# Fewer convolution taps behind each attention head group of block two's first layer, the rest behind the linear attention

## The chip, the cores and the metric

The kernel runs on one core of one Trainium2 chip. The metric is the device time of one execution in microseconds (us), as the median of several. The engines named below are TensorE (PE, its weight loads PEld), VectorE (DVE), ScalarE (ACT), GpSimd (POOL), and SyncE (SP), whose queue issues the loads.

## What is computed

Two blocks of two layers each work on a sequence of 256 tokens of width 1024; block two carries a second sequence of 256 context tokens along. The change touches layer 0 of block two. There, three branches read the same normalised input: a convolution of 31 taps over time with 512 channels, a gated linear attention (GLA, in chunks of 64), and a grouped attention of 8 heads. Three sigmoid gates merge them:

```python
def conv_module(val, glu, gate, dw_w, dw_b, ln_g, ln_b, w_o):
    u = val * jax.nn.sigmoid(glu)
    u = lax.conv_general_dilated(u, dw_w[:, None, :], ..., feature_group_count=D_CONV) + dw_b
    u = jax.nn.silu(layer_norm_2(u, ln_g, ln_b)) * jax.nn.silu(gate)
    return u @ w_o
...
    def merge(p, ya, yb, yc):
        return (jax.nn.sigmoid(p[13]) * ya + jax.nn.sigmoid(p[14]) * yb
                + jax.nn.sigmoid(p[15]) * yc) @ w_out
```

## The kernel before

Every product of two matrices is made of three matmuls (lines 163 to 165): weights and activations are split into a high and a low half, and high by high, high by low and low by high are added up in PSUM. A weight unit of 512 KB is loaded by SP into a raw tile (wr), ACT makes its high half (wh, line 133) and DVE its low half (wl, line 134). Units are loaded and split a few ahead of their use.

Layer 0 of block two runs over both sequences at once, 512 tokens. Its program order is: keys, queries and values of the attention; the convolution's inputs (up, four tiles of 128 channels); the attention, in eight groups (four blocks of 128 tokens, named at00 to at03, by two key heads), with the matmuls of GLA's keys, queries and values (f0GK, f0GQ, t0GV) and of the attention's output gate (f0ag) as filler; then the gate ag and the branch m3 with the attention's output weights oa; GLA in two passes (gl00 for the context, gl01 for the sequence); the gate gg and the branch m2 with GLA's output weights og; the end of the convolution (transposes cvt of ucv on, line 1316); the gate cg and the branch m1 with oc.

A branch works through four pairs of gates: two matmul groups f0m, then two output groups (yoa, yog, yoc), each added into acc by DVE. A gate such as gg has four parts; each ends in a product with the branch (qgg, line 1256), split into ygg0 (high, ACT) and ygg1 (low, DVE, line 199), which the matmuls of yog read.

The convolution is 124 DVE instructions in one chain: four tiles ucv of 31 taps, each tap reading and writing the same ucv (lines 989 and 991). They come from a generator, `taps`, and are given out in portions. A portion is only tied to stand behind its anchor, an instruction on the same engine:

```python
    def some_taps(n, anchor):
        for _ in range(n):
            t = next(taps, None)
            if t is not None:
                g.after(t, anchor)
```

The anchors are: for each attention group, the product that puts its row maxima in place (line 1033), with `TAPS[l]` taps; for each part of the gate ag and each merge of m3, `TAPG[l][0]` and `TAPG[l][1]`; for each part of the gate gg and each merge of m2, `TAPG[l][2]` and `TAPG[l][3]`. What is left is given out at the start of `conv_finish`. With 20 behind each group, six groups and a part of the seventh use up all 124, and the other portions of layer 0 find none. A scheduler in the framework fixes each engine's order when the program is built, from priorities that follow the program's order and from its own estimates; on the chip each engine works through its own list in that order.

Of the kernel before, what the change touches and what calls it, by code (L numbers as in the profile page):

```python
# [733 lines left out]

TAPS = (20, 19)
TAPG = ((0, 15, 5, 4), (3, 3, 14, 10))


def mod_stream(g, l, W):
# [74 lines left out]
def block2(g, l, hT, res_of, W, out=None, then=lambda x: None):  # L816
# [177 lines left out]
# [7 lines that stand above are left out]
    def scores(tb, kv):  # L1001
# [18 lines left out]
        for h in range(0, 4, n):  # L1020
# [5 lines left out]
            if h + n < 4:  # L1026
# [5 lines left out]
        nc.tensor.transpose(pm, ms.bitcast(F32).rearrange("p a h -> p (a h)"), idf)  # L1032
        some_taps(TAPS[l], nc.vector.tensor_mul(q2[64:72], pm[:, None, :].to_broadcast([8, 4, 128]),
                                                g.hm[0:8, :, None].to_broadcast([8, 4, 128])))
# [212 lines left out]
    def gate(n, f, q):  # L1247

        ps = fm(f'{n}{f}')
        tg = tgt(f'gt{n}{f}')  # L1250
        nc.scalar.activation(tg, ps, AF.Tanh, scale=0.5, bias=hb[:, blk(n, f)])
        nc.scalar.activation(q[:, f, :], ps, AF.Identity, bias=b_all[:, blk(n, f)])
        nc.vector.scalar_tensor_tensor(q[:, f, :], tg, 1.0, q[:, f, :], op0=OP.add, op1=OP.mult)

    def gated(f, q, src, y, scale, ntaps):
        nc.vector.tensor_mul(q[:, f, :], q[:, f, :], src)
        some_taps(ntaps, split_out(g, y[0][:, f, :], y[1][:, f, :], q[:, f, :], scale))
# [39 lines left out]
    def branch(bi, n, o, y, ntaps):  # L1297
        for i in range(4):
            merge(bi, o, i, [merge_gate(n, 2 * i + mb) for mb in range(2)], y, ntaps)

    def merge_gates(n):
        sg = k8('sg' + n, [128, 8, NT])
        return [merge_gate(n, f, sg[:, f, :]) for f in range(8)]

    def merges(bi, o, sg, y, ntaps):
        for i in range(4):
            merge(bi, o, i, sg[2 * i:2 * i + 2], y, ntaps)

    def conv_finish():
        for _ in taps:  # L1310
            pass
        ns = []
        for tb in range(NT // 128):
            pt = pp.tile([128, 4, 128], F32, name=f'cvt{l}{tb}', tag='at', bufs=g.AT)
            for f in range(4):
                nc.tensor.transpose(pt[:, f, :], ucv[f][:, 128 * tb:128 * tb + 128], idf)
            st = sp.tile([128, 6], F32, name=f'cvs{l}{tb}', tag='cvs', bufs=4)
            nc.vector.bn_stats(st, pt.rearrange("p f t -> p (f t)"))
            mv = sp.tile([128, 2], F32, name=f'cvm{l}{tb}', tag='cvm', bufs=4)
            nc.vector.bn_aggr(mv, st)  # L1320
            y = rsqrt(g, mv[:, 1:2], 1, 1.0, 1e-6, f'cv{l}{tb}')
            n = t2(f'cvn{tb}')
            nc.vector.tensor_scalar(n, pt.rearrange("p f t -> p (f t)"), mv[:, 0:1], y, op0=OP.subtract, op1=OP.mult)
            ns.append(n)
        for f in range(4):
            pt = pp.tile([128, NT], F32, name=f'cvb{l}{f}', tag='at', bufs=g.AT)
            for tb in range(NT // 128):
                nc.tensor.transpose(pt[:, 128 * tb:128 * tb + 128], ns[tb][:, 128 * f:128 * f + 128], idf)
            tz = t2(f'cvz{f}', NT)
            nc.scalar.activation(tz, pt, AF.Tanh, scale=g.hclg[l][:, f:f + 1], bias=g.hclb[l][:, f:f + 1])  # L1330
            nc.vector.tensor_scalar(ucv[f], pt, g.clg[l][:, f:f + 1], g.clb[l][:, f:f + 1], op0=OP.mult, op1=OP.add)
            nc.vector.scalar_tensor_tensor(ucv[f], tz, 1.0, ucv[f], op0=OP.add, op1=OP.mult)
# [7 lines left out]
    for f in range(4):  # L1340
        gate('ag', f, q)
        gated(f, q, aoT[:, f, :], y, 1.0, TAPG[l][0])
    if full:
        branch(0, 'm3', 'oa', y, TAPG[l][1])
    else:
        merges(0, 'oa', merge_gates('m3'), y, TAPG[l][1])
    if not full:
# [10 lines left out]
    if full:  # L1358
        q = k8('qgg', [128, 4, NT])
        y = pair('ygg', F32R)  # L1360
        for f in range(4):
            gate('gg', f, q)
            gated(f, q, goT[:, f, :], y, 1.0, TAPG[l][2])
        branch(1, 'm2', 'og', y, TAPG[l][3])
        conv_finish()
# [4 lines left out]
    else:  # L1370
        y = pair('ygg', F32R)
        for f in range(4):
            gated(f, q, goT[:, f, :], y, 1.0, TAPG[l][2])
        merges(1, 'og', sg, y, TAPG[l][3])
# [426 lines left out]
```

## Time and profile before

| what | value |
|---|---|
| median of the runs | 1201.55 us |
| lowest run | 1201.11 us |
| time of the profiled execution | 1202.12 us |
| its span, first to last instruction | 1200.3 us |
| busy PE, DVE, ACT | 1170.1, 919.0, 571.1 us |

The profiled execution lies 0.57 us above the median, and 1.8 us of its time lie outside the span. Times inside the trace count from the start of the span. A matmul is reported longer than the distance to the next one, since matmuls are pipelined: those of 512 columns take 0.39 us and follow each other every 0.23 us.

### The profile page before, as it was taken

The page shows a single profiled execution, that of the slowest core. Times are in us where ns is not written, and L with a number is a line of the kernel's source. Part 1 is how long each engine was busy: PE and PEld are TensorE (multiplying, and loading weights), DVE is VectorE, ACT ScalarE, POOL GpSimd, SP SyncE. Part 2 cuts the span into 40 slices and gives each one's busy share as a digit, 9 for nine tenths or more (in the row PEclk, how much of TensorE's full clock was granted, in tenths as well). Part 3 has the DMA queues.
Part 4 walks back from the last instruction along what each step waited for, and adds up shares of the span by engine and source line. Part 5 has one row for each costly group of instructions (what it writes and reads, how often), then busy time and mean ns, then how long its engine had stood idle before and what let it go on. Part 6 is the DMA issues. An engine that isn't in the chain of part 4 may idle for free.

```text
span 1200.3 us, 20616 instructions
## 1 busy us (share of the span) xinstructions
PE 1170.1 (97%) x8012; PEld 978.8 (82%) x8012; DVE 919.0 (77%) x2050; ACT 571.1 (48%) x1024; POOL 11.2 (1%) x42
## 2 busy tenths in 40 slices
PE   8999999999999999999799999999999999999998
PEld 6888766677887777778578888888999778999998
DVE  6986766966799759999946544845799897896984
ACT  5556534456565433246254522433455533855552
POOL 0000000000000000000000000000000000000000
PEclk9999999999999999999899999999999999999999
DMA  7643566466555642131131332334655333544552
GB/s 258 230 126 121 191 202 227 166 211 201 188 189 205 197 140 71 44 115 37 57 119 54 93 101 88 88 105 158 177 159 170 110 106 112 187 160 124 176 176 71
DMA packets 48258, 171.33 MB, mean 143 GB/s; under 512 B 5340, under 2 KB 6492, under 8 KB 47392
## 3 DMA queue, kind: packets, MB, share of 16 engines
q1 hardware_dynamic: 48160, 170.01, 43.5%
q8 instruction: 63, 1.03, 0.3%
q14 instruction: 35, 0.29, 0.1%
HBM read 167.89 MB, written 2.10 MB: 142 GB/s over the span
## 4 chain that ended last, share of the span: by engine, by line
PE 75%; DVE 13%; DMA 5%; ACT 4%; issue 2%; SPq 0%; ACTq 0%; DVEq 0%
PE f0m L163 3%; PE f0m L165 3%; PE f0m L164 3%; PE f1m L165 2%; PE f1m L163 2%; PE f1m L164 2%; PE mod L749 1%; PE po L164 1%; PE po L165 1%; PE po L163 1%; PE go L165 1%; PE go L164 1%; PE go L163 1%; DVE ucv L991 1%; PE yog L165 1%
## 5 line engine op out<-in xcount | busy, mean ns | idle before, releaser
L991 DVE SCALAR_TENSOR_TENSOR ucv<-up,par,ucv 128x512 f32<-128x512 f32 (+1 forms) x240 | 146.9, 612 | 2.1
L165 PE MATMUL f0m<-hTh,wl_0m 128*128 128x512 f32 x192 | 75.4, 393 | 0.0
L163 PE MATMUL f0m<-hTh,wh_0m 128*128 128x512 f32 x192 | 75.3, 392 | 0.0
L164 PE MATMUL f0m<-hTl,wh_0m 128*128 128x512 f32 x192 | 75.2, 392 | 0.0
L163 PE MATMUL f1m<-hTh,wh_1m 128*128 128x256 f32 x192 | 54.9, 286 | 0.1
L165 PE MATMUL f1m<-hTh,wl_1m 128*128 128x256 f32 x192 | 54.8, 286 | 0.0
L164 PE MATMUL f1m<-hTl,wh_1m 128*128 128x256 f32 x192 | 54.5, 284 | 0.0
L133 ACT CAST wh_0m<-wr_0m 128x1024 fp32r<-128x1024 f32 x24 | 25.3, 1054 | 58.1 <-PE f0m L164 15.7
L134 DVE TENSOR_TENSOR wl_0m<-wr_0m,wh_0m 128x1024 fp32r<-128x1024 f32 x24 | 29.2, 1220 | 21.6 <-ACT wh_0m L133 21.5
L165 PEld LDWEIGHTS f0m<-hTh,wl_0m 128*128 128x128 f32 x192 | 36.2, 189 | 7.7 <-issue 0.2
L164 PEld LDWEIGHTS f0m<-hTl,wh_0m 128*128 128x128 f32 x192 | 36.2, 189 | 7.4
L163 PEld LDWEIGHTS f0m<-hTh,wh_0m 128*128 128x128 f32 x192 | 36.2, 189 | 7.4
L163 PEld LDWEIGHTS f1m<-hTh,wh_1m 128*128 128x128 f32 x192 | 36.8, 192 | 0.5 <-ACT wh_1m L133 0.3
L165 PEld LDWEIGHTS f1m<-hTh,wl_1m 128*128 128x128 f32 x192 | 36.7, 191 | 0.2 <-DVE wl_1m L134 0.2
L164 PEld LDWEIGHTS f1m<-hTl,wh_1m 128*128 128x128 f32 x192 | 36.8, 191 | 0.1
L133 ACT CAST wh_1m<-wr_1m 128x1024 fp32r<-128x1024 f32 x24 | 25.0, 1050 | 24.4 <-PE f1m L164 9.8
L134 DVE TENSOR_TENSOR wl_1m<-wr_1m,wh_1m 128x1024 fp32r<-128x1024 f32 x24 | 29.3, 1219 | 8.6 <-ACT wh_1m L133 8.4
L1278 ACT ACTIVATE mtm<-f0m,hbin 128x512 f32<-128x512 f32 x24 | 16.4, 682 | 9.3 <-DVE acc L1291 8.9
L134 DVE TENSOR_TENSOR wl_0o<-wr_0o,wh_0o 128x1024 fp32r<-128x1024 f32 x8 | 9.8, 1224 | 13.2 <-ACT wh_0o L133 13.2
L1392 DVE SCALAR_TENSOR_TENSOR xT<-po,mod,xT 128x256 f32<-128x256 f32 x16 | 7.7, 483 | 14.6 <-PE po L165 14.6
L164 PE MATMUL yoa<-yag,wh_0oa 128*128 128x512 f32 x32 | 13.2, 414 | 5.3 <-DVE yag L199 5.3
L164 PE MATMUL po<-mgl,wh_0o 128*128 128x256 f32 x64 | 18.2, 285 | 0.0
(1854 smaller groups left out, 3971.6 us busy)
## 6 DMA issues: line engine op xcount, KB each, us to landing
wr_0mod<-in_wm_dram SPq DMA_DIRECT2D x24, 512.0 KB, 4.4
wr_1mod<-in_wm_dram SPq DMA_DIRECT2D x24, 512.0 KB, 3.6
wr_0m<-in_w_dram SPq DMA_DIRECT2D x24, 512.0 KB, 3.5
wr_1m<-in_w_dram SPq DMA_DIRECT2D x24, 512.0 KB, 3.5
wr_0O<-in_w1o_dram SPq DMA_DIRECT2D x8, 512.0 KB, 3.6
wr_1O<-in_w1o_dram SPq DMA_DIRECT2D x8, 512.0 KB, 4.1
wr_0o<-in_wo_dram SPq DMA_DIRECT2D x8, 512.0 KB, 3.5
wr_0p<-in_wo_dram SPq DMA_DIRECT2D x8, 512.0 KB, 3.7
```

What stands on the lines that cost most here:

```text
L133: g.nc.scalar.copy(wh, r)
L134: g.nc.vector.tensor_sub(wl, r, wh.bitcast(F32))
L163: nc.tensor.matmul(out, lh, rh, start=start, stop=False)
L164: nc.tensor.matmul(out, lh, rl, start=False, stop=False)
L165: nc.tensor.matmul(out, ll, rh, start=False, stop=stop)
L749: nc.tensor.matmul(ps[32 * q:32 * q + 32], g.cz[:, k // 2, 2 * (k % 2):2 * (k % 2) + 32], w[:, 0, 256 * q:256 * q + 256], start=k == 0, st ...
L991: yield nc.vector.scalar_tensor_tensor(o, src, dw[:, i, j:j + 1], o, op0=OP.mult, op1=OP.add)
L1278: nc.scalar.activation(sg, pm, AF.Tanh, scale=0.5, bias=hb[:, blk(n, f)])
L1392: nc.vector.scalar_tensor_tensor(r[:, f, :], ps[:, :256], g.mod[l][:, 16 + f, w:w + 1], r[:, f, :], op0=OP.mult, op1=OP.add)
```

## The change

Two lines of numbers:

```diff
-TAPS = (20, 19)
-TAPG = ((0, 15, 5, 4), (3, 3, 14, 10))
+TAPS = (10, 19)
+TAPG = ((0, 0, 6, 4), (3, 3, 14, 10))
```

Layer 0 now hands out 10 taps behind each of the eight attention groups (80), none behind the gate ag and the branch m3, 6 behind each of the four parts of gg (24), and 4 behind each merge of m2, of which five merges find some (20). Layer 1's numbers are the same. The scheduler makes new orders of this for layer 0. They differ on PE and DVE from the second attention group to the end of GLA's first pass, on ACT nearly as far; DVE differs again where the taps now stand. SP's order is the same, and one of POOL's memsets moves by one place.

DVE, first pass of GLA, before. gl001last to gl001qi are steps of the pass in the backward direction, yag1 is the low half of the last part of the gate ag, ucv03 a tap of the last convolution tile:

```order
L1137 COPY gl001last_6337<-gl001cum_6332 128x8
L991 SCALAR_TENSOR_TENSOR ucv03_4999<-up03_4597,par2_1328,ucv03_4999 128x512
L1142 TENSOR_TENSOR gl001ks_0_6341<-gl001last_6337,gl001cum_6332 128x512
L991 SCALAR_TENSOR_TENSOR ucv03_4999<-up03_4597,par2_1328,ucv03_4999 128x512
L199 SCALAR_TENSOR_TENSOR yag1_0_5665<-qag_0_5663,yag0_0_5664 128x512
L991 SCALAR_TENSOR_TENSOR ucv03_4999<-up03_4597,par2_1328,ucv03_4999 128x512
L1145 TENSOR_TENSOR gl001ks_0_6341<-gl001ks_0_6341,qkT_0_5380 128x512
```

DVE, the same place, after:

```order
L199 SCALAR_TENSOR_TENSOR yag1_0_5620<-qag_0_5618,yag0_0_5619 128x512
L134 TENSOR_TENSOR wl_0oa1_5888<-wr_0oa1_5781,wh_0oa1_5887 128x1024
L1177 COPY gw0_0_5616<-gl000c0_6262 128x256
L1180 SCALAR_TENSOR_TENSOR gw0_0_5616<-gw0_0_5616,gl000dec_6243,gl000c1_6263 128x128 x2
L1180 SCALAR_TENSOR_TENSOR gw0_0_5616<-gw0_0_5616,gl000dec_6243,gl000c0_6262 128x128 x2
L1180 SCALAR_TENSOR_TENSOR sts0_5612<-gw0_0_5616,gl000dec_6243,gl000c1_6263 128x128 x2
L1137 COPY gl001last_6292<-gl001cum_6287 128x8
L1142 TENSOR_TENSOR gl001ks_0_6296<-gl001last_6292,gl001cum_6287 128x512
```

The taps between the steps are gone, and yag1's last part stands ahead of the pass's first chain of states (line 1180) and no longer in the second direction.

PE, first pass of GLA, before. yoa00 to yoa02 are output groups of branch m3, which read yag; f0m3_2 and f0m3_3 are gates of the same branch:

```order
L163 MATMUL f0m3_2_5970<-hTh0_0_3338,wh_0m3_2_5866 128x512
L164 MATMUL f0m3_2_5970<-hTl0_0_3340,wh_0m3_2_5866 128x512
L163 MATMUL f0m3_3_6003<-hTh0_0_3338,wh_0m3_3_5899 128x512
L164 MATMUL f0m3_3_6003<-hTl0_0_3340,wh_0m3_3_5899 128x512
L163 MATMUL yoa02_6036<-yag0_0_5664,wh_0oa1_5932 128x512
L164 MATMUL yoa02_6036<-yag1_0_5665,wh_0oa1_5932 128x512
L164 MATMUL yoa00_5936<-yag1_0_5665,wh_0oa0_5828 128x512
L165 MATMUL yoa00_5936<-yag0_0_5664,wl_0oa0_5829 128x512
L164 MATMUL yoa01_5950<-yag1_0_5665,wh_0oa0_5828 128x512
L1155 MATMUL gl001ktp_6351<-cst_66,gl001ks_0_6341 128x128 x4
```

PE, the same place (the transposes gl001ktp), after:

```order
L164 MATMUL f0m3_1_5858<-hTl1_0_3341,wh_0m3_1_5745 128x512
L165 MATMUL f0m3_1_5858<-hTh1_0_3339,wl_0m3_1_5746 128x512
L163 MATMUL yoa00_5891<-yag0_0_5619,wh_0oa0_5783 128x512
L1155 MATMUL gl001ktp_6306<-cst_66,gl001ks_0_6296 128x128 x4
L164 MATMUL yoa00_5891<-yag1_0_5620,wh_0oa0_5783 128x512
L165 MATMUL yoa00_5891<-yag0_0_5619,wl_0oa0_5784 128x512
```

Before, PE had started six groups of branch m3 by this place; now the second direction's transposes stand behind the first matmul of yoa00, and all of yoa00, yoa01, f0m3_2 and f0m3_3 stand behind them.

DVE, the gate gg, before:

```order
L199 SCALAR_TENSOR_TENSOR ygg1_0_6740<-qgg_0_6738,ygg0_0_6739 128x512
L134 TENSOR_TENSOR wl_0og0_6858<-wr_0og0_6741,wh_0og0_6857 128x1024
L1253 SCALAR_TENSOR_TENSOR qgg_0_6738<-gtgg1_0_6810,qgg_0_6738 128x512
L1256 TENSOR_TENSOR qgg_0_6738<-qgg_0_6738,goT_0_6264 128x512
L199 SCALAR_TENSOR_TENSOR ygg1_0_6740<-qgg_0_6738,ygg0_0_6739 128x512
L134 TENSOR_TENSOR wl_0m2_2_6896<-wr_0m2_2_6779,wh_0m2_2_6895 128x1024
```

DVE, the gate gg, after:

```order
L199 SCALAR_TENSOR_TENSOR ygg1_0_6695<-qgg_0_6693,ygg0_0_6694 128x512
L991 SCALAR_TENSOR_TENSOR ucv02_5159<-up02_4532,par2_1328,ucv02_5159 128x512 x3
L134 TENSOR_TENSOR wl_0og0_6832<-wr_0og0_6696,wh_0og0_6831 128x1024
L991 SCALAR_TENSOR_TENSOR ucv02_5159<-up02_4532,par2_1328,ucv02_5159 128x512
L1253 SCALAR_TENSOR_TENSOR qgg_0_6693<-gtgg1_0_6771,qgg_0_6693 128x512
L991 SCALAR_TENSOR_TENSOR ucv02_5159<-up02_4532,par2_1328,ucv02_5159 128x512
L1256 TENSOR_TENSOR qgg_0_6693<-qgg_0_6693,goT_0_6219 128x512
L991 SCALAR_TENSOR_TENSOR ucv02_5159<-up02_4532,par2_1328,ucv02_5159 128x512
L199 SCALAR_TENSOR_TENSOR ygg1_0_6695<-qgg_0_6693,ygg0_0_6694 128x512
```

Taps now stand between the steps of the gate: eleven between the first part's low half and the fourth part's first step, three more ahead of the fourth part's low half. The last tap of all stands behind the sixth merge of m2, ahead of the last two.

## Rows read from the trace of the kernel before

**Rows 1.** The page: busy time by engine, and the chain that ended last.

```profile
PE 1170.1 (97%) x8012; PEld 978.8 (82%) x8012; DVE 919.0 (77%) x2050; ACT 571.1 (48%) x1024; POOL 11.2 (1%) x42
...
PE 75%; DVE 13%; DMA 5%; ACT 4%; issue 2%; SPq 0%; ACTq 0%; DVEq 0%
```

**Rows 2.** Busy time by stretch: PE, PEld, DVE, ACT, POOL, granted clock, DMA.

```profile
475.00:500.00 25.00, 24.99 (x196) 19.51 (x194) 23.94 (x41) 7.22 (x12) 1.05 (x2) 1.00 0.01 1
...
550.00:575.00 25.00, 21.46 (x132) 17.49 (x130) 24.09 (x44) 14.31 (x24) 0.00 (x0) 0.99 0.08 22
575.00:600.00 25.00, 20.04 (x196) 16.41 (x197) 25.00 (x40) 6.06 (x10) 0.17 (x2) 0.81 0.24 68
```

**Rows 3.** Who PE waited for, 420 to 700: total, times, longest.

```profile
PE yoa L164 <- DVE yag L199: 5.3, 1, 5.3
PE gl00o L1217 <- DVE gl00am L1209: 3.0, 2, 1.8
PE gn00t L1242 <- DVE gw L1239: 0.7, 1, 0.7
PE gl01a L1201 <- DVE gw L1180: 0.6, 1, 0.6
PE gn01t L1242 <- DVE gw L1239: 0.3, 1, 0.3
PE gl001c L1166 <- ACT gl001kt L1157: 0.2, 1, 0.2
```

**Rows 4.** Busy time by stretch of 2 us around the longest wait, columns as in Rows 2.

```profile
574.00:576.00 2.00, 0.00 (x0) 0.00 (x0) 2.00 (x6) 0.71 (x2) 0.00 (x0) 0.63 0.00 0
576.00:578.00 2.00, 1.28 (x3) 0.85 (x4) 2.00 (x5) 1.10 (x3) 0.00 (x0) 0.50 0.00 0
...
584.00:586.00 2.00, 2.00 (x8) 1.59 (x8) 2.00 (x6) 0.00 (x0) 0.00 (x0) 0.81 0.55 213
...
592.00:594.00 2.00, 1.45 (x14) 1.33 (x16) 2.00 (x3) 0.00 (x0) 0.00 (x0) 1.00 0.00 0
```

**Rows 5.** Timeline of PE: the matmuls on both sides of the longest wait.

```profile
571.07 0.39 PE L164 MATMUL yoa<-yag,wh_0oa 128*128 128x512 f32 x1
576.72 0.79 PE L164 MATMUL yoa<-yag,wh_0oa 128*128 128x512 f32 x1 [5.26 <-DVE yag L199]
```

**Rows 6.** The chain that ended last, first pass of GLA: start, us, what.

```profile
568.75 0.66 DVE ucv L991
...
581.12 1.14 DVE wl_0m L134
...
590.04 0.66 DVE ucv L991
...
595.29 0.69 DVE gl00am L1209
```

**Rows 7.** Busy time of the taps' line 991 alone: DVE, clock, DMA.

```profile
440.00:600.00 160.00, 89.37 (x120) 0.97 0.21 64
600.00:665.00 65.00, 0.00 (x0) 1.00 0.27 88
665.00:750.00 85.00, 0.00 (x0) 1.00 0.31 93
```

**Rows 8.** Busy time by stretch, gate gg and branch m2, columns as in Rows 2.

```profile
665.00:675.00 10.00, 10.00 (x47) 8.32 (x48) 6.17 (x8) 4.80 (x8) 0.00 (x0) 1.00 0.36 105
675.00:685.00 10.00, 10.00 (x46) 8.29 (x45) 6.02 (x8) 5.65 (x8) 0.00 (x0) 1.00 0.31 85
...
sum 70.00, PE 70.00 PEld 58.03 DVE 31.68 ACT 23.60 POOL 0.00; mean PE 10.00 PEld 8.29 DVE 4.53 ACT 3.37 POOL 0.00
```

**Rows 9.** Timelines of DVE and PE: the fourth part of gg, and what reads it.

```profile
682.65 0.69 DVE L1253 SCALAR_TENSOR_TENSOR qgg<-gtgg,qgg 128x512 f32<-128x512 f32 x1
684.76 0.69 DVE L199 SCALAR_TENSOR_TENSOR ygg<-qgg,ygg 128x512 fp32r<-128x512 f32 x1 [0.70 <-ACT ygg L198]
...
693.57 0.39 PE L164 MATMUL yog<-ygg,wh_0og 128*128 128x512 f32 x1
...
745.72 1.47 PE L1316 MATMUL cvt<-cst,ucv 128*128 128x128 f32 x12
```

**Rows 10.** Who DVE waited for, attention, 440 to 560: the longest two.

```profile
DVE at030mx L1025 <- PE at030s L1024: 1.0, 1, 1.0
DVE at011mx L1025 <- PE at011s L1024: 0.9, 2, 0.5
```

**Rows 11.** The page: loads of the gates' weights, KB each, us to landing.

```profile
wr_0m<-in_w_dram SPq DMA_DIRECT2D x24, 512.0 KB, 3.5
```

## The prediction

> **What bounds the kernel now.** I read the page first: PE is busy 97% of the span and holds 75% of the chain that ended last, so the kernel is bound by PE nearly everywhere, and a change to DVE's work can only pay where PE stands still [rows 1]. The table of busy time by stretch shows where that is. In the middle of the attention, 475 to 500, PE is busy 24.99 of 25 us although DVE is at 23.94; there the taps cost nothing. From 550 to 600 PE has 21.46 and 20.04 of 25, and DVE 24.09 and 25.00: here DVE is the bound [rows 2]. The list of PE's waits names the places: 5.3 us for the low half of the gate ag, 3.0 us in two waits for GLA's masked scores, 0.7 and 0.2 us more in the first pass, against 0.6 and 0.3 in the second pass, which runs without taps [rows 3]. The chain of waits says what DVE was doing meanwhile: from 568.75 to 590.04 it runs on DVE and alternates between the steps of GLA and taps; between 568.75 and 595.98, where the last of it ends, I count 20 whole taps of 0.66 us, 13.2 us [rows 6]. All taps but those of the second layer run before 600, none later [rows 7].
>
> The long wait has a second cost. PE stands still from 571.07 to 576.72, and the first matmul behind it takes 0.79 us, the one ahead of it 0.39 [rows 5]. The granted clock falls during the wait, stands at 0.50 (the level of 1.2 GHz), and is back at 1.00 after about 585 [rows 4].
>
> **What the change does, part by part.**
>
> *Taps taken out of the attention and the first pass.* 80 of the 124 stay ahead of the gate ag, 44 go. In DVE's new order no tap stands between the end of the attention and the gate gg, so the 20 that sat on the chain in the first pass are gone, and with them the backlog that held back yag. PE's waits of the first pass go: 5.3 + 3.0 + 0.7 + 0.2 = 9.2 us [rows 3].
>
> *The clock.* Without the long wait I expect no fall: the waits of 1.8 us and 1.2 us (the rest of 3.0) after it left the clock at 1.00 [rows 3, 4]. PE worked at half clock from 576.72 until the clock rose; the mean of 0.81 in 584 to 586 puts the rise at 584.76. That is 8.0 us, less the 0.2 us wait inside it: 7.8 us of work that would take 3.9 [rows 3 to 5]. So 3.9 us come back. The Trainium skill ("TensorE: Matmul & The Clock Gate", section Terms) puts the penalty at the whole throttled time times the missing share of the clock. By the means of 0.63 and 0.81 the clock was low from 574.52 to 584.76, 10.2 us, so by that rule 5.1 us come back. I take the row's 3.9, since in the first 2.2 of those 10.2 us PE had nothing to run [rows 4, 5].
>
> *What is late next.* With DVE free, PE's own work sets the pace of the first pass, in the new order in which GLA's steps are spread among whole gates of m3. The trace has no such run of the first pass; the nearest is the second pass, the same code without taps, where PE waited 0.6 + 0.3 = 0.9 us [rows 3]. I add back 0.9. Below that, nothing (0.0); above it, the first pass's waits for scores and norms, 3.0 + 0.7 = 3.7, if they are the latency of the chain and not the taps.
>
> *The attention's new order.* PE now reaches each score and exponent with some matmuls of filler fewer in between. The trace of before shows DVE waiting for PE in the attention, up to 1.0 us, and PE for nobody [rows 3, 10]. I take 0. A gain is excluded, since PE is full there [rows 2]; a loss is bounded by that 1.0 us turned round in each of the six groups whose order changes, 6.0 us.
>
> *Taps put behind the gate gg.* They are hidden by PE's matmuls if DVE keeps up. Between 665 and 735 DVE is busy 31.68 of 70 us, and 44 taps of 0.66 are 29.0, together 60.7 of 70 [rows 6, 8]. The tight place is the gate itself, where DVE is at 6.17 and 6.02 of 10. From 664.7 to 682.65, 17.9 us, DVE has some 10.9 us of its own and receives eleven taps, 7.3: 18.2, less the split of one weight unit (1.14) which has moved behind: 17.1, so there is hardly any backlog [rows 6, 8, 9]. Behind 682.65 stand one tap that may be under way, two more and the first tap of the next tile (four of 0.66 at most, 2.6), that split, and three steps of at most 0.69: 2.6 + 1.1 + 2.1 = 5.8. The fourth low half is then ready at about 688.5, and PE wants it at 693.57: 5 us to spare [rows 6, 9]. If that cover is gone, each further tap costs PE 0.66. The waiting queue of DVE at this place holds the splits of m2 and og weights; they are used one to three matmul groups later. ACT's high halves ygg0 wait for qgg, which is inside the same sum.
>
> *The end of the convolution.* The last tap stands behind the sixth merge of m2, the transposes cvt start at 745.72, and the taps of that merge have the two merges behind it, about 15 us, to end [rows 9]. Cost 0. Layer 1, SP's loads and PE's order from the second pass on stay as they are: 0.
>
> **The sum.** 9.2 + 3.9 - 0.9 = 12.2 us. The profiled execution took 1202.12 us, and would take 1189.9; it lies 0.57 above the median, so the forecast is 1201.55 - 12.2 = 1189.4 us. The chain seen from DVE gives the same size (13.2 us of taps on it), which is the same stretch from the other side and no second proof.
>
> **The rivals.**
>
> *The wait moves to the weights.* Between 562 and 582 the loads rest (DMA share 0.00 in 574 to 576), because raw tiles wait to be split; they run again behind 582 [rows 4]. If PE comes through 12 us earlier, the units of m3 must too. For it speaks that a load takes 3.5 us to land [rows 11]; against it, that DVE and ACT, which free the raw tiles, are freed by the same change: ACT is busy only 6.06 of 25 us in that stretch [rows 2]. Two loads a whole landing late cost 7.0: 1196.4 us. A first pass that keeps its 3.7 us instead of 0.9, or an attention that gives up a few microseconds, ends near there too.
>
> *The throttled time counts whole.* If the clock's fall also held up what follows through the first 2.2 us, 5.1 come back instead of 3.9, and the time is 1188.2; with no wait left in the first pass, 1187.3. The page's rule in the part on the clock would give this. Against it stands that DVE, not PE, ended the chain in that stretch [rows 6].
>
> *The attention turns against the change (slower).* PE's order is fixed, so a score or exponent that isn't ready when its turn comes stops all filler behind it. If each of the six groups waits 3 us, that is 18, and the time is 1201.55 + 18 - 12.2 = 1207.4. It decides from 12.2 / 6 = 2.0 us a group. Against it: twice the longest wait that DVE shows there, and DVE has fewer taps between the steps than before [rows 10].
>
> *The gate gg becomes the bound.* It decides from 5 us of lateness, eight taps more than the order puts there. If all 24 taps of the gate stood ahead of the fourth low half, ten more, PE would wait 1.6 us: 1191.0. It is inside the forecast's own range.
>
> *The change does nothing.* It would take the new numbers to be without effect in the order; the order shows 10 taps a group and the others behind gg and m2, so I give this none.
>
> **How the numbers follow.** Forecast as summed, 1186 to 1193: 0.62. Smaller gain, 1193 to 1200: 0.20. Larger gain, down to 1184, the rule's rival included: 0.12. Slower than before: 0.06. The range reaches from 1184 to 1198, which leaves out the slower case and the end of the smaller gain. A measurement of this kernel tells about 2% from no change, 24 us: faster than 1177.5 would need twice the sum (0.02); slower than 1225.6 needs over 6 us a group in the attention (0.02); within, 0.96.
>
> **What the profile after would show.** PE's waits in the first pass fall below 2 us in all, and none is above 1.5; the granted clock is 1.00 from 560 to 600; the first pass ends about 12 us earlier while the second pass and all behind it keep their lengths. Line 991 has about 77 instructions before the first pass and 43 between the gate gg and the sixth merge, none on the chain; DVE's 31.68 us there become about 60. The low half of gg's fourth part ends about 5 us ahead of its reader. I am wrong if PE waits for exponents or maxima in the attention, for wl or wh of m3 in the first pass, or for ygg.

## The result, and the profile after

The changed kernel takes 1192.42 us (median of 6, 1190.20 to 1193.95). The kernel before, in three further executions, took 1206.71 to 1209.78 us; of its six, one of 2284.37 us is far outside the rest and in no ratio, and the other five have a median of 1206.71. The ratio is 0.989, interval 0.9857 to 0.9923: 1.1% faster, and inside the 2% that I called no change. The forecast was 1189.4 in a range of 1184 to 1198.

The two profiled executions are 1202.12 us before and 1191.59 after, 10.5 apart. First the page of the changed kernel, busy time by engine and the chain that ended last; it answers to [rows 1].

```profile
PE 1166.4 (98%) x8012; PEld 975.8 (82%) x8012; DVE 920.7 (77%) x2050; ACT 569.7 (48%) x1024; POOL 11.2 (1%) x42
...
PE 74%; DVE 12%; DMA 6%; ACT 5%; issue 2%; SPq 0%; ACTq 0%; DVEq 0%
```

DVE does the same work, 920.7 us against 919.0; PE is busy 3.7 us less with the same 8012 instructions, most of it where the half clock has gone (2.9 us, below). Busy time by stretch (PE, PEld, DVE, ACT, POOL, clock, DMA) says where; it answers to [rows 2, 4]:

```profile
475.00:500.00 25.00, 24.93 (x194) 19.22 (x193) 23.05 (x41) 7.11 (x12) 1.05 (x2) 1.00 0.07 18
...
550.00:575.00 25.00, 24.90 (x227) 20.37 (x226) 20.21 (x39) 14.70 (x24) 0.00 (x0) 1.00 0.30 91
575.00:600.00 25.00, 24.32 (x154) 20.20 (x153) 10.66 (x23) 9.74 (x25) 0.00 (x0) 1.00 0.21 62
```

PE has 24.90 and 24.32 of 25 us where it had 21.46 and 20.04, the clock is 1.00 throughout, and DVE's 24.09 and 25.00 have become 20.21 and 10.66. Who PE waited for from 420 to 700, in total, times, longest; it answers to [rows 3]:

```profile
PE at031e L1045 <- ACT at031x L1048: 1.1, 1, 1.1
PE gn00t L1242 <- DVE gw L1239: 0.7, 1, 0.7
PE gl01a L1201 <- DVE gw L1180: 0.6, 1, 0.6
PE gn01t L1242 <- DVE gw L1239: 0.3, 1, 0.3
```

The waits for yag and for the masked scores are gone. One is new, in the last attention group. ACT's timeline (start, us) shows what stood in its way there:

```profile
539.03 1.05 ACT L133 CAST wh_0oa<-wr_0oa 128x1024 fp32r<-128x1024 f32 x1 [1.87 <-DMA wr_0oa<-in_wa_dram]
539.98 2.05 ACT L1048 ACTIVATE at031x<-at031e 128x512 f32<-128x512 f32 x4
```

PE's timeline shows what it cost:

```profile
540.63 0.50 PE L1045 MATMUL at031e<-at031q,k 128*128 128x512 f32 x1 [1.13 <-ACT at031x L1048]
```

ACT's list has the high half of a weight unit ahead of the exponents. ACT stood 1.87 us until that unit had landed, the exponents came behind it, and PE waited for the first of them.

Where the time was gained can be read between two steps that both kernels have: the first of all taps (line 989, on DVE), ahead of which the two orders are the same, and the first matmul z of GLA's second pass (line 1119, on PE). Their timelines in the changed kernel:

```profile
439.42 0.55 DVE L989 TENSOR_SCALAR ucv<-up,par 128x512 f32<-128x512 f32 x1
614.78 0.40 PE L1119 MATMUL z<-w,lrT 98*128 98x512 f32 x1
```

Busy time between them (columns as above):

```profile
439.42:614.78 175.36, 173.39 (x1293) 135.69 (x1293) 137.15 (x234) 74.41 (x129) 3.24 (x7) 1.00 0.24 76
```

The same two steps in the kernel before:

```profile
439.88 0.55 DVE L989 TENSOR_SCALAR ucv<-up,par 128x512 f32<-128x512 f32 x1
625.42 0.40 PE L1119 MATMUL z<-w,lrT 98*128 98x512 f32 x1
```

And busy time there:

```profile
439.88:625.42 185.54, 176.28 (x1293) 138.88 (x1293) 164.32 (x278) 74.81 (x129) 3.41 (x9) 0.97 0.23 72
```

The stretch is 10.2 us shorter: PE's idle time in it went from 9.26 to 1.97 us (7.3), its busy time for the same 1293 matmuls from 176.28 to 173.39 (2.9). With the 0.5 us by which the first tap itself came earlier, z comes 10.6 us earlier. The transposes cvt come at 735.05 after 745.72, 10.7 earlier, so the second pass, the gate gg and branch m2 neither give nor take. There the taps are, and line 991 says how many; it answers to [rows 7] (DVE, clock, DMA):

```profile
440.00:570.00 130.00, 57.42 (x77) 1.00 0.24 78
570.00:652.00 82.00, 0.00 (x0) 1.00 0.23 70
652.00:690.00 38.00, 18.68 (x25) 1.00 0.28 86
690.00:750.00 60.00, 13.49 (x18) 1.00 0.32 97
```

### The profile page after: what moved, and what is told of

It is laid out like the page before. It is cut to its first block, busy times and chain, and to the rows that moved or that the text cites. A ratio compares the mean times of both kernels' runs of the same rounds, so it can differ in the third digit from the quotient of the medians.

```text
span 1189.8 us, 20622 instructions
## 1 busy us (share of the span) xinstructions
PE 1166.4 (98%) x8012; PEld 975.8 (82%) x8012; DVE 920.7 (77%) x2050; ACT 569.7 (48%) x1024; POOL 11.2 (1%) x42
## 4 chain that ended last, share of the span: by engine, by line
PE 74%; DVE 12%; DMA 6%; ACT 5%; issue 2%; SPq 0%; ACTq 0%; DVEq 0%
PE f0m L165 4%; PE f0m L164 3%; PE f0m L163 3%; PE f1m L165 2%; PE f1m L163 2%; PE f1m L164 2%; PE mod L749 1%; PE po L164 1%; PE po L165 1%; PE po L163 1%; PE go L165 1%; PE go L164 1%; PE go L163 1%; PE yog L165 1%; PE yoc L165 1%
## 5 line engine op out<-in xcount | busy, mean ns | idle before, releaser
L134 DVE TENSOR_TENSOR wl_0o<-wr_0o,wh_0o 128x1024 fp32r<-128x1024 f32 x8 | 9.8, 1223 | 13.2 <-ACT wh_0o L133 13.2
L163 PE MATMUL pp<-mgh,wh_0p 128*128 128x256 f32 x64 | 18.2, 284 | 0.0
L165 PE MATMUL pp<-mgh,wl_0p 128*128 128x256 f32 x64 | 18.2, 284 | 0.0
```

The source lines that it names most:

```text
L134: g.nc.vector.tensor_sub(wl, r, wh.bitcast(F32))
L163: nc.tensor.matmul(out, lh, rh, start=start, stop=False)
L165: nc.tensor.matmul(out, ll, rh, start=False, stop=stop)
```

## The experiments

All times are medians; the ratio is to the kernel before on the same chip. The kernel before ran beside e1 to e4, beside e5 to e8 and beside e9 to e12, each time on another chip. Where traces are compared, the spans' zeros differ by some us, so times are counted from the first tap.

| run | taps behind each attention group | us | ratio, interval |
|---|---|---|---|
| e1 | 10, rest behind m3 | 1193.51 | 0.9909, 0.9877 to 0.994 |
| e2 | 10, rest left out | 1192.17 | 0.9899, 0.9868 to 0.993 |
| e3 | 8 | 1189.72 | 0.9876, 0.9845 to 0.9907 |
| e4 | 6 | 1191.50 | 0.9889, 0.9852 to 0.9926 |
| e5 | 20, 8 extra matmuls | 1203.92 | 0.9995, 0.9981 to 1.0009 |
| e6 | 20, 20 extra matmuls | 1205.34 | 1.0009, 0.9999 to 1.0018 |
| e7 | 15 | 1199.56 | 0.997, 0.9956 to 0.9985 |
| e8 | 13 | 1190.91 | 0.989, 0.9866 to 0.9913 |
| e9 | 20 (kernel before) | 1203.08 | 0.9986, 0.997 to 1.0002 |
| e10 | 10 (changed kernel) | 1192.16 | 0.9899, 0.9878 to 0.9919 |
| e11 | 8 | 1190.44 | 0.9883, 0.9862 to 0.9904 |
| e12 | 10, rest behind ag | 1192.90 | 0.9904, 0.9883 to 0.9925 |

**e1, half of the change.** Against the changed kernel:

```diff
-TAPG = ((0, 0, 6, 4), (3, 3, 14, 10))
+TAPG = ((0, 15, 5, 4), (3, 3, 14, 10))
```

> Half of the change: 10 taps behind each attention group, but the second row of numbers as before, so the other 44 go behind the merges of branch m3. In DVE's order none of them stands ahead of the masked scores of the first pass of GLA, about ten stand among the norm's steps of that pass, the rest up to the second pass. Theory (a tap costs only where DVE is the bound and PE waits behind it): the attention and the first pass up to its outputs run as in the changed kernel, the granted clock stays at 1.00, the wait for the normed output of the first pass grows from 0.7 us by 2 to 6 us: 1194 to 1199 us. Rival A (the gain comes from the attention, where both have the same 10 taps): as the changed kernel, 1192 us within 1. Rival B (any tap left in the first pass gives the whole gain back): 1202 us or more.

Measured: 1193.51 us, the changed kernel's time within the intervals, and no wait for the norm of the first pass at all. PE's timeline shows why:

```profile
594.12 0.63 PE L1242 MATMUL gn00t<-cst,gw 128*128 128x128 f32 x4
```

In the changed kernel that transpose starts at 588.87, after its wait. With the taps among the norm's steps the scheduler has put it further back in PE's list, and PE gets there without waiting. My 2 to 6 us took PE's order as given, and it isn't: new numbers give a new order on PE too. The second row of numbers, where the 44 taps go, is worth nothing by itself that these runs can tell.

**e2, the moved taps left out.** In the generator of the changed kernel, which leaves the last two tiles of the convolution incomplete:

```diff
+                if l == 0 and 31 * i + j >= 80 and j:
+                    continue
```

> The changed kernel with 43 taps of layer 0 left out, those that stand behind the gate gg and the merges of m2 (the last two tiles of the convolution are incomplete). Theory (they lie beside PE's matmuls and cost nothing): the time of the changed kernel, 1192.4 us within 1.0. Rival (they take something from PE or from the splits there): faster by more than 1 us; at most 43 x 0.66 = 28 us.

Measured: 1192.17, no gain over the changed kernel's 1192.42. The 43 taps behind the gate and the merges are free.

**e3 and e4, fewer in the attention.**

```diff
-TAPS = (10, 19)
-TAPG = ((0, 0, 6, 4), (3, 3, 14, 10))
+TAPS = (8, 19)
+TAPG = ((0, 0, 9, 6), (3, 3, 14, 10))
```

> 8 taps behind each attention group, 9 behind each part of gg, 6 behind each merge of m2. Theory (the first pass has no backlog at 10 and so has none to lose at 8): the time of the changed kernel, 1191.0 to 1193.5 us; the 1.1 us wait for an exponent in the last attention group is ACT's and stays or moves. Rival (DVE still holds the attention back at 10): faster by 1 to 3 us. Rival (the gate gg becomes the bound with 16 more taps behind it): PE waits for ygg, slower by 1 us or more.

> 6 taps behind each attention group, 10 behind each part of gg, 6 behind each merge of m2: in DVE's order the last four taps and two weight splits stand behind the first step of the last merge, and PE's transposes cvt of the convolution follow its last output group at once. Theory (a tap without cover costs its full time): PE waits at cvt for 4 x 0.66 + 2 x 1.2 + 2 x 0.69 = 6.4 us, and if the granted clock falls in that wait, some 3 us more: 1197 to 1203 us. Rival (a wait there is taken up by other matmuls or shorter, since taps run ahead): 1192 to 1194 us.

Measured: 1189.72 and 1191.50. With 8 the wait for an exponent in the last group is gone, and no wait for ygg has come. So the gain was the one of the first rival's size, though not by its reason: the exponent was held by ACT and a load, not by DVE. With 6, I had forecast a wait of 6.4 us at cvt. The trace of e4 has these transposes:

```profile
738.70 1.14 PE L1316 MATMUL cvt<-cst,ucv 128*128 128x128 f32 x9
749.45 0.55 PE L1316 MATMUL cvt<-cst,ucv 128*128 128x128 f32 x3 [0.52 <-DVE ucv L991]
```

The three that read the late tile have been put 10.7 us behind the nine others, among the matmuls of the gate cg, and wait 0.52 us. The expectation was wrong in the same way as in e1.

**e5 and e6, PE kept at work in the longest wait.** In the kernel before, with 8 and with 20:

```diff
             py = pp.tile([128, 512], F32, name=f'y{o}{l}{f}', tag='gm', bufs=g.GM)
+            for _ in range(20 if l == 0 and o == 'oa' and f == 2 else 0):
+                nc.tensor.matmul(py[:, :NT], wh[:, 0, 0:128], y[0][:, 0, :], start=True, stop=True)
             for k in range(4):
```

> The kernel before, with 8 extra matmuls on PE: the first product of output group yoa02 is started over 8 times more, with the same operands, right ahead of the longest wait. Every other instruction of every engine stands where it stood. They take 8 x 0.23 = 1.8 us out of an idle stretch of 5.65. Theory (the idle PE lets the clock fall, and the half clock behind it is on the path): if the clock holds with 3.8 us of idle time left, the kernel gains up to the 3.9 us that I gave the clock, 1198 us; if it falls all the same, nothing, as before on the same chip. Rival (DVE's chain of taps ends that stretch whatever PE's clock): no change within 1 us, and what PE gains it waits for the masked scores.

> The same with 20 extra matmuls, 4.6 us, which leaves about 1 us of idle time (one step of GLA changes places with a neighbour on PE, nothing else moves). Theory: the granted clock stays at 1.00, its mean over the run goes from 0.987 to 0.995 in the kernel before to 0.998 or more, and although PE has more to do the time falls to 1197 to 1200 us in every run, without the spread of the kernel before on the same chip (1200.5 to 1211.9). Rival (DVE's chain ends the stretch whatever the clock): 1201 us or more, with longer waits of PE for the masked scores.

Measured: 1203.92 and 1205.34, the time of the kernel before both times. In e5 the clock fell all the same (a mean of 0.68 in 574 to 576), so it says nothing about the clock. In e6 the first wait has shrunk, by who PE waited for:

```profile
PE gl00o L1217 <- DVE gl00am L1209: 3.9, 1, 3.9
PE f0m L165 <- DVE wl_0m L134: 0.8, 1, 0.8
PE yoa L164 <- DVE yag L199: 0.7, 1, 0.7
```

and the clock holds where it fell before, by busy time in stretches of 2 us (columns as above):

```profile
576.00:578.00 2.00, 1.44 (x6) 0.92 (x7) 2.00 (x4) 0.87 (x2) 0.00 (x0) 1.00 0.00 0
...
590.00:592.00 2.00, 0.00 (x0) 0.00 (x0) 2.00 (x4) 0.00 (x0) 0.17 (x2) 1.00 0.00 0
592.00:594.00 2.00, 1.68 (x8) 1.68 (x8) 2.00 (x4) 0.00 (x0) 0.00 (x0) 0.51 0.00 0
598.00:600.00 2.00, 2.00 (x18) 1.77 (x18) 2.00 (x3) 0.05 (x1) 0.00 (x0) 0.50 0.68 236
604.00:606.00 2.00, 2.00 (x6) 1.57 (x6) 0.00 (x0) 1.88 (x10) 0.00 (x0) 0.58 0.37 152
```

PE comes through the stretch at full clock and is stopped one step later, for 3.9 us at the masked scores, since DVE (busy 2.00 of 2 us) has come no further. In that wait the clock falls after all, and stays at 0.50 until about 605.7. This second fall costs time of its own (e9 below), so e6's time alone does not tell what the first was worth; DVE's timeline of e6 does:

```profile
575.75 0.68 DVE L199 SCALAR_TENSOR_TENSOR yag<-qag,yag 128x512 fp32r<-128x512 f32 x1
595.06 0.68 DVE L1209 TENSOR_TENSOR gl00am<-gl00am,gl00am 128x512 f32<-128x512 f32 x1
```

From yag's last low half to the second masked score DVE takes 19.3 us here at PE's full clock, and 19.3 in the kernel before, whose clock is low for the first half of it (575.98, shown with e8, to 595.29 [rows 6]). The rival of these two runs held: with DVE's chain as it was, PE's clock in the middle of it is worth nothing.

**e7 and e8, the number of taps on DVE's chain.**

```diff
-TAPS = (20, 19)
-TAPG = ((0, 15, 5, 4), (3, 3, 14, 10))
+TAPS = (13, 19)
+TAPG = ((0, 0, 3, 2), (3, 3, 14, 10))
```

and (15, 19) with (0, 0, 1, 0) for e7.

> 15 taps behind each attention group, 1 behind each part of gg for the 4 that are left. In DVE's order 23 taps still stand in the first pass ahead of the masked scores (26 in the kernel before, none in the changed one). Theory (what counts is how many taps stand on DVE's chain in the first pass): as the kernel before, 1199 to 1206 us, with the wait for yag of 4 us or more and the clock falling. Rival (the time goes by the taps per attention group, half way between 20 and 10): 1196 to 1198 us.

> 13 taps behind each attention group, 3 behind each part of gg, 2 behind each merge of m2. In DVE's order 8 taps stand between the first steps of the two directions of the first pass, none behind. Theory: 8 x 0.66 = 5.3 us of DVE's time, which meet the slack that DVE has there without taps, so PE waits 0 to 4 us and the clock stays at 1.00: 1191 to 1196 us. Rival (the time goes by the taps per attention group): 0.3 of the way from 10 to 20, 1195 to 1197 us, without a wait in the first pass.

Measured: 1199.56 and 1190.91. Counted from the first step gl000last to the first product of the masked scores (line 1207), DVE's order has 27 taps in the kernel before (the prediction counted the 20 of the chain behind 568.75), 24 in e7 and 8 in e8. Ahead of yag's last low half are 15, 15 and 8 of them. Who PE waited for in e7, from 420 to 760, the two longest:

```profile
PE yoa L164 <- DVE yag L199: 5.3, 1, 5.3
PE gl00o L1217 <- DVE gl00am L1209: 0.6, 1, 0.6
```

With as many taps ahead of yag as in the kernel before, e7 has the same wait for it; with three fewer behind it, the wait for the masked scores is nearly gone, and the kernel gains 0.3%. The same list of e8, whole:

```profile
PE gl01a L1201 <- DVE gw L1180: 0.6, 1, 0.6
PE f0m L165 <- DVE wl_0m L134: 0.5, 1, 0.5
PE gn01t L1242 <- DVE gw L1239: 0.3, 1, 0.3
PE gn00t L1242 <- DVE gw L1239: 0.3, 1, 0.3
```

e8 is the run that decides. As built, its order on PE is that of the kernel before up to and past the matmul of the longest wait, and on DVE up to the middle of the first pass; its attention is that of the kernel before. What it lacks from there on are 19 of the 27 taps, 7 of them ahead of yag's last low half; DVE's other steps close up, and that low half moves ahead of one of them (line 1142). DVE's timeline has that step. In the kernel before:

```profile
575.98 0.68 DVE L199 SCALAR_TENSOR_TENSOR yag<-qag,yag 128x512 fp32r<-128x512 f32 x1
```

In e8, with its first tap:

```profile
437.63 0.55 DVE L989 TENSOR_SCALAR ucv<-up,par 128x512 f32<-128x512 f32 x1
568.43 0.68 DVE L199 SCALAR_TENSOR_TENSOR yag<-qag,yag 128x512 fp32r<-128x512 f32 x1
```

In the changed kernel:

```profile
560.37 0.68 DVE L199 SCALAR_TENSOR_TENSOR yag<-qag,yag 128x512 fp32r<-128x512 f32 x1
```

Counted from the first tap, PE of the kernel before has nothing left but this from 131.4 us on (571.3 [rows 5]). There the step ends at 136.8, in e8 at 131.5 and in the changed kernel at 121.6. 131.5 is just in time and 136.8 is not; whatever lies further ahead, as 121.6, buys nothing: from the first tap to z e8 takes 174.1 us (z at 611.77), the changed kernel 175.4. e8 has the whole gain of the change without its attention, so the gain does not come from the attention. The rival that goes by the taps per group (1195 to 1197) is out.

**e9, the kernel before once more.**

> The kernel before once more, for a second profile of it. Its times spread from 1200.3 to 1206.4 us on the last chip, with mean granted clocks of 0.995 down to 0.988. Theory (the waits on DVE's chain let the clock fall a second time, behind the waits for the masked scores, where PE is the bound again and the half clock costs its full half): an execution with a clock of 0.991 shows a second stretch at 0.50 between 588 and 605, and its excess over 1200.5 us is about half of that stretch. Rival (the spread comes from the loads at the start of the kernel): the profile differs ahead of 440 us, and the clock between 560 and 610 is as in the first profile.

Measured: 1200.96 to 1206.21 us, the profiled execution 1206.21 with a mean clock of 0.989. It has the first profile's wait of 5.3 us and one of 3.4 for the masked scores (3.0 in two there), but not its clock:

```profile
574.00:576.00 2.00, 0.00 (x0) 0.00 (x0) 2.00 (x6) 0.21 (x1) 0.00 (x0) 0.63 0.00 0
580.00:582.00 2.00, 1.75 (x29) 1.44 (x32) 2.00 (x4) 0.51 (x1) 0.00 (x0) 0.67 0.00 0
590.00:592.00 2.00, 0.00 (x0) 0.00 (x0) 2.00 (x5) 0.00 (x0) 0.17 (x2) 0.89 0.00 0
...
598.00:600.00 2.00, 2.00 (x12) 1.77 (x12) 2.00 (x2) 0.95 (x2) 0.00 (x0) 0.50 0.56 193
600.00:602.00 2.00, 2.00 (x30) 1.95 (x26) 1.24 (x2) 0.00 (x0) 0.00 (x0) 0.55 0.75 229
```

It falls twice, at about 574.5 and again in the wait for the masked scores, and is low from 591.6 to 601.8, 10.2 us. The timelines of this execution have the end of that wait, the second masked score and z:

```profile
593.22 2.07 PE L1217 MATMUL gl00o<-gv,gl00am 128*128 128x128 f32 x8 [3.43 <-DVE gl00am L1209]
595.95 0.69 DVE L1209 TENSOR_TENSOR gl00am<-gl00am,gl00am 128x512 f32<-128x512 f32 x1
628.89 0.40 PE L1119 MATMUL z<-w,lrT 98*128 98x512 f32 x1
```

The second masked score comes 0.66 us later than in the first profile (595.29 [rows 6]), a difference that is there ahead of the attention already; z comes 3.47 later. So the second fall cost 2.8 us, and not the half of 10.2: PE had nothing to run until 593.22, and the first profile's second wait of 1.2 us is gone. The first profile has only the first fall [rows 4]; of the 4.1 us that this execution took more, the second fall explains those 2.8. The first low stretch ended sooner here, at 581.3 instead of 584.8, and what PE gained by it went into the wait, 3.4 us where the first profile has 1.8. In the seven executions of the kernel before beside e1 to e4 the clock goes with the time: 1200.54 us at 0.995, 1204.49 at 0.991, 1211.87 at 0.987. How much of that is the second fall, no trace of them says; the mean also counts other stretches, as 0.86 in the first 25 us of e9.

**e10 to e12.** The changed kernel again, 8 taps again, and the changed kernel with its 44 taps behind the gate ag:

```diff
-TAPG = ((0, 0, 6, 4), (3, 3, 14, 10))
+TAPG = ((11, 0, 0, 0), (3, 3, 14, 10))
```

> The changed kernel once more, beside the next two on the same chip: 1190 to 1194 us, as before.

> 8 taps behind each attention group, as in the run with 8 above, on the same chip as the changed kernel. Theory (it has lost the 1.1 us wait for an exponent in the last attention group and 0.4 us of the wait for the norm): 1.0 to 2.0 us faster than the changed kernel. Rival (the difference between the two was one of chips): equal within 0.5 us.

> 10 taps behind each attention group as in the changed kernel, but the other 44 behind the parts of the gate ag: in DVE's order 13 of them stand in the first pass ahead of its masked scores, 5 among these, and the rest among the norm's steps and later. The attention is left as in the changed kernel up to its last group. Theory (only taps on DVE's chain in the first pass cost, less the slack that DVE has there): 18 x 0.66 = 11.9 us on the chain, of which the slack takes some 5: PE waits 3 to 7 us more in the first pass, 1194 to 1200 us. Rival A (the gain of the change came from the attention's 10 taps): 1192 us within 1.

Measured: 1192.16, 1190.44 and 1192.90. Eight is 1.7 us faster than ten by the medians, and the intervals of the two overlap (0.9862 to 0.9904, 0.9878 to 0.9919). By the traces the stretch from the first tap to z takes 173.5 us with 8 (e3 and e11) and 175.4 and 174.9 with 10 (the changed kernel and e10), so the difference is likely real; none of the waits for an exponent of 1.1 and 0.6 us is in e3 or e11. e12 missed what I expected by my theory. Its busy time in the first pass:

```profile
560.00:575.00 15.00, 14.89 (x158) 12.28 (x154) 14.67 (x31) 5.38 (x9) 0.00 (x0) 1.00 0.17 48
575.00:590.00 15.00, 15.00 (x133) 12.76 (x129) 14.43 (x22) 5.28 (x18) 0.00 (x0) 1.00 0.19 60
590.00:605.00 15.00, 14.93 (x70) 12.04 (x69) 14.38 (x29) 5.42 (x10) 0.00 (x0) 1.00 0.45 140
```

DVE is at 43.5 of 45 us, as full as in the kernel before, with 18 taps ahead of and among the masked scores, and PE waits for none of it. The taps per group alone would say the same of this run, and e8 has ruled that out. So it isn't the number of taps in the first pass either, but whether DVE comes to the steps that PE reads before PE does: counted from the first tap, e12 has yag's last low half done at 128.5 us, 8.3 ahead of the kernel before, and PE's list has the outputs gl00o at 141.1, where the changed kernel has them at 137.3, and the norm's transposes later still.

## Why the prediction was right, and where it was off

*What bounds the kernel now.* Right: DVE's backlog in the first pass of GLA stopped PE, and nowhere else did taps cost (e2, e8). PE's waits in the first pass fell to 0.7 us and the clock stayed at 1.00, as forecast; z came 10.6 us earlier where I had about 12.

*Taps taken out.* I took off 9.2 us of waits and added back 0.9. 0.7 is left, the norm's, so 8.5 us went where I had 8.3. (571.07 is the start of the last matmul ahead of the longest wait and not of the wait itself; the 5.3 us that I summed are the row's.)

*The clock.* This term was too large: 3.9 us forecast, 2.9 measured as PE's busy time for the same matmuls. Why 7.8 us of work at half clock cost less than half, no run separates. As bookkeeping of PE's own time it was sound: idle time plus lost clock, and both went. As a cause of its own it was not; e6 took the first fall away and got nothing, because DVE's chain ended the stretch. The page of the Trainium skill that I weighed ("TensorE: Matmul & The Clock Gate", section Terms) would have had 5.1; the measured 2.9 is further from that than from my 3.9. What a low clock costs was decided by which engine ended the stretch: in the first fall it was DVE, and nothing came back for the clock alone (e6); in the second of e9 it was PE, and 8.6 us of work at half clock (593.2 to 601.8) cost 2.8, with a wait of 1.2 us that went away taken off.

*The attention's new order.* This step failed. I took 0 and bounded it by 6.0; it costs 1.1 us (0.6 in e10's trace of the same kernel), for an exponent behind a weight cast that waits for its load. A wait for exponents was one of the signs of being wrong that I had named. It is the rival of the weights in small, in the attention and not in the first pass. 8.5 + 2.9 - 1.1 = 10.3, and the stretch from the first tap to z became 10.2 shorter; my 12.2 is 2.0 too large, nearly all of it here and in the clock's 1.0.

*The gate gg and the end of the convolution.* Right. Line 991 has 77 and 43 instructions, as forecast. DVE is busy 59.7 us in the seventy that answer to [rows 8] (655 to 725; 60.7 forecast). The fourth low half ends at 676.5, the matmul that reads it starts at 682.91: 6.4 us to spare where I had 5. The last tap starts at 720.87, 14 us ahead of cvt.

*The time.* The forecast of 1189.4 lies 3.0 us below the median: 1.7 since the profiled executions lie 10.5 apart and not 12.2; 0.8 since the changed kernel's profiled execution is below its median by that; and 0.6 since I put that of the kernel before above its median by that, and there too it was one of the shorter. The gain by ratio, 1.1%, is 13.3 us of 1206.71, more than my 12.2, although the sum was too large: I had costed the profiled execution of the kernel before, which has one fall of the clock, and e9's has two. That these two errors nearly cancel is luck. From the first tap to z, the backlog's price is 10.2 us by the first profile of the kernel before and some 13 by e9's.

What stays open: why the scheduler's list put PE at yag's product ahead of a DVE that was 5 us late. That its own estimates were off there is likely, and no run shows it.

## What to carry to other kernels

A backlog on a filler engine costs nothing until it is late for the first step that the bound engine reads; from there its instructions cost most of their time (e8 lacks 20 taps of the first pass, 13.2 us, and is 11.4 us shorter from the first tap to z), so look for that step's finish time and PE's arrival, not for the busy share (e12: 43.5 of 45 us, no wait). Idle time and lost clock of one engine may be added up when their common cause goes, but taking one of them away alone gives nothing while another engine's chain ends the stretch. When numbers of a schedule change, expect the other engines' orders to move as well: three of my waits were priced on an order that was no longer there.

## What the runs showed of the hardware

At the same place in the same program, the granted clock fell in a wait of 3.4 us (e9, at the masked scores) and stayed at 1.00 through waits of 1.8 and 1.2 [rows 3, 4]. Work behind the wait does not bring it back at once: in e6 PE was at work again from 592.3 on, and the clock stood at 0.50 until about 605.7; behind the first wait the low stretch was 10.2 us long in the first profile and 6.8 in e9. An engine that is given a higher clock ahead of a step that another engine sets only waits longer for it (1.8 us became 3.4 in e9 and 3.9 in e6), and in both the clock fell in that longer wait. The spread of the kernel before, 1200.54 to 1211.87 us beside e1 to e4, goes with the mean clock, and the second fall explains 2.8 us of it in e9; but executions at 0.998 to 1.000 spread too, by 6.5 us in e11 (1187.94 to 1194.43).
